# The conditioning's chunk sums: from multiply-adds on three engines to fp32 products on TensorE

## The chip, the cores and the metric

The kernel runs on one core of a Trainium2 chip. The metric is the device time of one execution in microseconds. The engines are called as the profile calls them: PE is TensorE's products and PEld its weight loads, DVE is VectorE, ACT is ScalarE, POOL is GpSimd, SP is SyncE (it issues nearly all DMAs here).

## The reference, cut to what matters

One layer of a hybrid decoder over 1024 tokens of 2048 features, all in fp32:

```python
mod = jax.nn.silu(c) @ w_ada[layer] + b_ada[layer]      # c: (1, 2048), w_ada: (2048, 6144)
shift, scale, gate = jnp.split(mod, 3, axis=-1)
h = rms_norm(x, norm_gain[layer]) * (1.0 + scale[:, None, :]) + shift[:, None, :]
proj = h @ w_in[layer]                                   # 2048 x 8192
...                                                      # eight stick-breaking, eight retention heads
y = jnp.concatenate([oa, ob], axis=-1) @ w_out[layer]
x = x + gate[:, None, :] * y
```

The change concerns the first line, for the columns of the shift and the scale: a vector of 2048 numbers times 2048 x 4096 weights, 33.5 MB that are read once.

## The kernel before, in words

**Projections.** h.T stands in SBUF in 16 blocks (kc) of 128 features by two halves (hf) of 512 tokens. Each block is kept as two exact parts, h_hi and h_lo, and so is each tile of weights (hi: a rounded copy by ScalarE, lo: the difference, by VectorE or GpSimd). `mm3` (L132 to L135) makes three products of the parts: hi hi, lo hi, hi lo.

**Order.** TensorE's order is the program's (`manual_schedule`); a scheduler orders the other engines. SyncE's queue of DMAs waits, in its own order, for the buffers that its loads fill.

**Start.** x's first four blocks of tokens are loaded, squared (L241), scaled (L257, L259) and transposed (`x_turn`, L267, copied out at L269 or L271). Meanwhile w_ada arrives in chunks of 256 columns, four tiles a chunk (`load_ada`, tag "ada", nine buffers that it shares with the raw weights of `start_w`): chunks 0 to 7 are the scale, 8 to 15 the shift. A partition p holds 16 rows of a chunk.

**Chunk sums.** `ada_sums(cc)` weighs a partition's 16 rows with silu(c) and adds them. Row 0 goes to acc_p on ScalarE (L280). Six rows (`ADA_ACT`) are scaled in place by ScalarE (L282) and added to acc_p by GpSimd (L283). Nine go to acc_d on VectorE (L285, L287), which adds acc_p at the end (L288). `ada_mod(cc)` then sums over the partitions with two products of acc_d's columns with ones (L299), and VectorE makes of that two blocks' scale (L302, L303) or shift (L305).

**First products.** `make_h(kc, hf)` makes h.T without its shift (L311 on ScalarE, L316 on VectorE). `start_w(kc)` loads a block's weights for the first seven retention heads' z and splits them: two of three low parts on GpSimd, the others on VectorE (L347). `start_mm` multiplies them into seven banks (tiles "first", half 0). In the loop over kc, the next chunk's sums stand at odd kc and `ada_mod` behind the fifth head at even kc. From kc = 10 on, transposes of x's second half go in between, in the bank "C" that mod uses as well.

**Shift.** `shifts()` runs as a task between the steps of seven projections (`unit_t`, tiles "pj_rz", half 1): load a chunk, sum it, `SHIFT_GAP` = 6 steps later `ada_mod`, then `shift_h` for two blocks of half 0. `shift_h` adds the shift (L321), rounds (L323) and takes the low part (L327, odd kc on GpSimd). After the last of these projections `shift_h` runs for half 1, while q of the first head ("pj_q") is projected. From there on come the heads and the output projection, which the change doesn't touch. `gate_part` (L501) sums the gate's columns under the heads: one fp32 product of ones (32 columns) with a 128x256 tile.

Of the kernel before, what the change touches and what calls it, by code (L numbers as in the profile page):

```python
# [11 lines left out]
F32 = mybir.dt.float32  # L12
F32R = mybir.dt.float32r
I32 = mybir.dt.int32
AF = mybir.ActivationFunctionType
ALU = mybir.AluOpType

P = 128
# [22 lines left out]
NZ = 7  # L41
ADA_BUFS = 9
ADA_ACT = (2, 4, 7, 9, 12, 14)
SHIFT_GAP = 6
# [11 lines left out]
def layer_kernel(ctx, tc, x, c, w_ada, b_ada, norm_gain, w_in, sb_q_gain, sb_k_gain, ret_norm_gain, w_out,  # L56
                 rot, ret_mask, ret_kdec, chunk_decay, out):
    nc = tc.nc
# [12 lines left out]

# [1 line left out]
    ident = cons.tile([P, P], F32, name="ident")  # L73
# [33 lines left out]
    def rsqrt_newton(y, m, u, iters=3):  # L107
        """y = m ** -0.5 from the exponent trick and Newton's iteration (u is room for a product)."""
        nc.vector.tensor_scalar(y.bitcast(I32), m.bitcast(I32), -0.5, RSQRT_MAGIC, op0=ALU.mult, op1=ALU.add)
        for _ in range(iters):  # L110
            nc.vector.tensor_tensor(u, y, y, op=ALU.mult)
            nc.vector.scalar_tensor_tensor(u, u, -0.5, m, op0=ALU.mult, op1=ALU.mult)
            nc.vector.scalar_tensor_tensor(y, u, 1.5, y, op0=ALU.add, op1=ALU.mult)

# [1 line left out]
    def split_w(raw, name, lo_eng=nc.vector):  # L116
# [19 lines left out]

    h_hi, h_lo = {}, {}  # by block of 128 features and half of the tokens

    def unit_t(col0, halves, name, lo_pool=()):
        """(w_in[:, col0:col0+128]).T @ h.T, 512 tokens a bank. Yields between its steps; returns the banks."""  # L140
        o = {hf: ps.tile([P, HALF], F32, tag="pj", bufs=4, name=f"pj_{name}_{hf}") for hf in halves}
        for kq in range(4):
            def parts(raw):
                yield raw.rearrange("p (k n) -> p k n", n=P), w_in_k[:, 4 * kq:4 * kq + 4, col0:col0 + P]
            with tc.high_priority(AHEAD):
                hi, lo = wchunk(parts, f"{name}_{kq}", nc.gpsimd if kq in lo_pool else nc.vector)
            for hf in halves:
                for k in range(4):
                    kc = 4 * kq + k
                    sl = slice(k * P, (k + 1) * P)  # L150
                    mm3(o[hf], hi[:, sl], lo[:, sl], h_hi[kc, hf], h_lo[kc, hf], kc == 0, kc == KC - 1)
                    if k % 2:
                        yield
        return o

    def unit_v(col0, name):
        """h @ w_in[:, col0:col0+256]: two heads' values, two blocks of tokens a bank."""
        o = [ps.tile([P, HALF], F32, tag="pj", bufs=4, name=f"pv_{name}_{b}") for b in range(4)]
# [16 lines left out]

    # The projections are TensorE's steady work; the heads' tasks put their small products between
    # its steps, each some steps after the one whose results it needs.
    tasks = []
# [28 lines left out]

# [1 line left out]
    # The conditioning's scale is loaded before its shift. Until the shift is known h.T stands without it,  # L209
    # and what is projected from that (the first NZ retention heads' z) gets its share later (z_bias).  # L210
    ada_rows = w_ada[0].rearrange("(p j) n -> p j n", j=16)
# [6 lines left out]
    with tc.tile_pool(name="st", bufs=1) as st:  # L218
# [7 lines left out]
        def load_ada(cc, gs=range(4)):  # L226
            """A chunk of 256 columns of w_ada: eight chunks of the scale, then eight of the shift."""
            col = (D if cc < 8 else 0) + (cc % 8) * 2 * P
# [15 lines left out]
        def x_scale(ts, ss):  # L244
            """x over its rows' root mean squares, for some blocks of tokens."""
            n = len(ts)
# [14 lines left out]
        def x_turn(kc, g, tag, bufs):  # L261
            """Half of a block of x.T, into the place that the next block of h.T's low part takes over."""
            xT[kc, g] = hp.tile([P, HALF], F32, tag=f"hl{kc}_{g}", name=f"xT{kc}_{g}")
# [8 lines left out]

        def ada_sums(cc):
            """Sums of silu(c) w_ada over a partition's sixteen rows, for a chunk of 256 columns."""
            acc_d, acc_p = [st.tile([P, 256], F32, tag=f"acc_{n}", bufs=2, name=f"acc_{n}_{cc}") for n in "dp"]
            for j in range(16):
                src = ada[cc, j // 4][:, j % 4]
                cj = silu_c[:, j:j + 1]
                if j == 0:
                    nc.scalar.activation(acc_p, src, AF.Copy, scale=cj)  # L280
                elif j in ADA_ACT:
                    nc.scalar.activation(src, src, AF.Copy, scale=cj)  # L282
                    nc.gpsimd.tensor_tensor(acc_p, acc_p, src, op=ALU.add)  # L283
                elif j == 1:
                    nc.vector.tensor_scalar(acc_d, src, cj, None, op0=ALU.mult)  # L285
                else:
                    nc.vector.scalar_tensor_tensor(acc_d, src, cj, acc_d, op0=ALU.mult, op1=ALU.add)  # L287
            nc.vector.tensor_tensor(acc_d, acc_d, acc_p, op=ALU.add)  # L288
            return acc_d

# [4 lines left out]
        def ada_mod(cc, acc):  # L295
            """Sums over the partitions: (scale + 1) gain, or shift, for two blocks of h.T."""
            mod = ps.tile([P, 2], F32, tag="C", name=f"mod_{cc}")
# [9 lines left out]
        def make_h(kc, hf):  # L307
            """h.T without its shift."""
            a, xT_kc = mods[:, kc:kc + 1], xT.pop((kc, hf))
# [9 lines left out]
        def shift_h(kc, hf):  # L319
# [4 lines left out]
            if kc == 0:  # L324
                h_lo[kc, hf] = hp.tile([P, HALF], F32R, tag=f"hl15_{hf}", name=f"h_lo0s_{hf}")
            eng = nc.gpsimd if kc % 2 else nc.vector
            eng.tensor_tensor(h_lo[kc, hf], h32, h_hi[kc, hf].bitcast(F32), op=ALU.subtract)  # L327

        starter_tags = [("A0", 1), ("A1", 1), ("B", 1)] + [("pj", 4)] * 4
        first = {}  # L330

        def start_w(kc):
# [3 lines left out]
            for i in range(2):  # L336
# [8 lines left out]
                nc.scalar.activation(hi[:, 0:n], cols, AF.Copy)  # L345
                eng = nc.gpsimd if (2 * kc + i) % 3 else nc.vector
                eng.tensor_tensor(lo[:, 0:n], cols, hi[:, 0:n].bitcast(F32), op=ALU.subtract)  # L347
                ws.append((hi, lo))
# [84 lines left out]
        def shifts():  # L433
            for cc in range(8, 16):
                if 8 < cc < 15:
                    load_ada(cc + 1)
                if cc > 8:
                    sums[cc] = ada_sums(cc)
                    yield SHIFT_GAP
# [11 lines left out]

# [1 line left out]
    hd = ctx.enter_context(ExitStack())  # L453
# [30 lines left out]
    def gate_part(h, pool):  # L484
        """The gate's columns 256 h to 256 (h + 1), without their bias, to gate_row."""
        n = 2 * P
# [21 lines left out]
    def z_bias():  # L508
        """The shift's share in the first NZ retention heads' z, to zb."""
        acc = r_tile("zb_acc")  # L510
# [23 lines left out]

# [1 line left out]
    eps_c = cons.tile([P, 1], F32, name="eps_c")  # L536
# [29 lines left out]
    def split_r(r, name):  # L566
        """A tile's two exact parts, by halves."""
        parts = [com.tile([P, S], F32R, tag="R", bufs=6, name=f"{n}_{name}") for n in ("rh", "rl")]
        return parts

    def spill_v(o, h, pool):
        """Two heads' values to DRAM, as they stand in the banks."""
        with tc.high_priority(AHEAD):
# [7 lines left out]
    def sb_attention(h, q, k, pool, gap):  # L581
        # The heads' steps: a block of 128 queries over a chunk of 512 keys. Two blocks of queries
        # go together into the product with the values.
        steps = [(0, ib, 0) for ib in range(4)]
# [54 lines left out]
        def turn(s):  # L639
            """Transposes into banks of two blocks of keys by two blocks of queries; after the second, splits."""  # L640
            half, ib, ch = steps[s]
# [61 lines left out]
    with tc.tile_pool(name="sb", bufs=1) as sb:  # L703
# [19 lines left out]

        # The first retention head's queries and keys, under the last stick-breaking head.
        o = steady(unit_t(4 * GW, (0, 1), "rq0"))
# [6 lines left out]

# [1 line left out]
    c_hi, c_lo = {}, {}  # L734
# [14 lines left out]
    def out_unit(n, tbs, name, finish, half=None, tail=2):  # L749
        """y[:, 512 n:512 (n + 1)] for some blocks of tokens, a bank each (half: of concat, to be loaded too)."""  # L750
        o = {t: ps.tile([P, HALF], F32, tag=banks[t][0], bufs=banks[t][1], name=f"y_{name}_{t}") for t in tbs}
# [28 lines left out]
    with tc.tile_pool(name="rt", bufs=1) as rt:  # L780
# [147 lines left out]

# [1 line left out]
        start(ret_attention(NH - 1, q, k, vs.pop(NH - 1), z, 2))  # L930
# [80 lines left out]
```

## Time and profile before

| | |
|---|---|
| timed runs | 2153.45, 2157.64, 2159.12 us; median 2157.64 |
| profiled execution, first to last instruction | 2156.7 us |
| its whole time | not given apart from its span; the timed median is 0.9 us above the span |
| PE busy | 2066.9 us (96%) |
| DVE, ACT, POOL busy | 1212.4 (56%), 744.9 (35%), 340.0 us (16%) |
| mean granted clock of TensorE | 0.989 |
| moved by DMA | 224.29 MB, 104 GB/s over the span |

How to read it: the profile has a row of busy time for each engine. The span in 40 slices is shown by digits, tenths of a slice. A group has its line, engine, operation, the tile it writes and those it reads, their shapes, its count, then busy time, the mean of one in ns, and the idle time of the engine just before them with what ended it. A row of waits has the waiting instruction, what ended the wait, the total in us, the number of waits and the longest. A row of the timeline has its start, its length, and the instruction. Products are pipelined, so a row of PE is longer than the time that it occupies the engine. A row of one tile has shortest, median and longest duration and the first and last start. A row of stages has the stage, its length, the busy time of each engine, the granted clock, the share of the DMA engines' time and GB/s.

### The profile page before, as it was taken

The numbers are of one execution on the slowest core, as the hardware profiler recorded it, in microseconds if no ns is written. First come the engines' busy times: TensorE is split into PE (matmuls) and PEld (weight loads), VectorE is DVE, ScalarE is ACT, GpSimd is POOL, SyncE is SP. The second block draws the span as 40 slices with busy tenths as digits, with TensorE's granted clock in tenths as the row PEclk, the third lists the DMA queues.
The fourth block names the chain that finished last, engine by engine and source line by source line (L and its number), as shares of the span: only waits on it lengthen the run. The fifth ranks groups of instructions, "written<-read, shape, count | busy, mean of one in ns | idle before, by whom it ended". The sixth has DMA issues, their size and how long they took to land.

```text
span 2156.7 us, 29735 instructions
## 1 busy us (share of the span) xinstructions
PE 2066.9 (96%) x11167; PEld 1771.6 (82%) x11167; DVE 1212.4 (56%) x2270; ACT 744.9 (35%) x1424; POOL 340.0 (16%) x475
## 2 busy tenths in 40 slices
PE   4878899999999999999999999999999999999998
PEld 3656779888988898888988988988988988688887
DVE  6999774477448653865386556556355146523132
ACT  6655442444235433543254222223232123311110
POOL 3654330111011201120111101011011010000000
PEclk9989999999999999999999999999999999999999
DMA  8847511221222112121212533433232124734132
GB/s 281 297 153 231 181 49 59 79 69 45 64 69 74 50 59 74 56 62 59 74 50 77 168 117 96 132 97 115 89 96 62 54 62 146 223 104 132 49 127 78
DMA packets 232404, 224.29 MB, mean 104 GB/s; under 512 B 12674, under 2 KB 187844, under 8 KB 232260
## 3 DMA queue, kind: packets, MB, share of 16 engines
q1 hardware_dynamic: 231872, 222.36, 32.8%
q8 instruction: 87, 1.43, 0.3%
q14 instruction: 57, 0.47, 0.1%
q10 hardware_dynamic: 388, 0.04, 0.0%
HBM read 194.03 MB, written 28.32 MB: 103 GB/s over the span
## 4 chain that ended last, share of the span: by engine, by line
PE 73%; DVE 13%; DMA 5%; issue 4%; ACT 3%; POOL 1%; ACTq 0%; SPq 0%; DVEq 0%; POOLq 0%
PE y L134 4%; PE y L135 4%; PE y L133 4%; PE pv_v L135 3%; PE pv_v L134 3%; PE pv_v L133 3%; PE pj_rq L133 3%; PE pj_rq L135 3%; PE pj_rq L134 3%; PE pj_rk L133 3%; PE pj_rk L135 3%; PE pj_rk L134 3%; PE pj_q L134 2%; PE pj_z L133 2%; PE pj_q L133 2%
## 5 line engine op out<-in xcount | busy, mean ns | idle before, releaser
L133 PE MATMUL pv_rv<-wh_rv,h_hi 128*128 128x256 f32 x512 | 146.5, 286 | 3.5 <-ACT wh_rv L119 3.5
L133 PE MATMUL y<-wh_o,c_hi 128*128 128x512 f32 x384 | 149.4, 389 | 0.0
L134 PE MATMUL y<-wl_o,c_hi 128*128 128x512 f32 x384 | 149.4, 389 | 0.0
L135 PE MATMUL y<-wh_o,c_lo 128*128 128x512 f32 x384 | 149.4, 389 | 0.0
L134 PE MATMUL pv_rv<-wl_rv,h_hi 128*128 128x256 f32 x512 | 146.1, 285 | 0.8 <-DVE wl_rv L121 0.7
L134 PE MATMUL pv_v<-wl_v,h_hi 128*128 128x256 f32 x512 | 144.9, 283 | 0.0
L133 PE MATMUL pv_v<-wh_v,h_hi 128*128 128x256 f32 x512 | 144.9, 283 | 0.0
L135 PE MATMUL pv_rv<-wh_rv,h_lo 128*128 128x256 f32 x480 | 136.4, 284 | 0.0
L135 PE MATMUL pv_v<-wh_v,h_lo 128*128 128x256 f32 x480 | 135.8, 283 | 0.0
L121 DVE TENSOR_TENSOR wl_o<-wr_o,wh_o 128x512 fp32r<-128x512 f32 x48 | 33.2, 692 | 180.3 <-ACT wh_o L119 180.3
L632 DVE TENSOR_TENSOR_SCAN om<-om 128x128 f32<-128x128 f32 (+2 forms) x96 | 96.2, 1002 | 43.6 <-POOL om L622 42.3
L119 ACT ACTIVATE wh_o<-wr_o 128x512 fp32r<-128x512 f32 x48 | 30.3, 632 | 220.7 <-PE y L135 216.3
L133 PEld LDWEIGHTS pv_rv<-wh_rv,h_hi 128*128 128x128 f32 x512 | 98.8, 193 | 4.9 <-ACT wh_rv L119 3.9
L133 PE MATMUL pj_rq<-h_hi,wh_rq 128*128 128x512 f32 x256 | 102.6, 401 | 0.3 <-ACT v L469 0.3
L133 PE MATMUL pj_rk<-h_hi,wh_rk 128*128 128x512 f32 x256 | 102.3, 400 | 0.0
L283 POOL TENSOR_TENSOR acc_p<-acc_p,ada 128x256 f32<-128x256 f32 x96 | 87.0, 907 | 96.9 <-ACT ada L282 68.0
L133 PE MATMUL pj_z<-h_hi,wh_z 128*128 128x512 f32 x256 | 101.3, 396 | 0.0
L133 PE MATMUL pj_q<-h_hi,wh_q 128*128 128x512 f32 x256 | 100.7, 393 | 0.0
L135 PE MATMUL pj_q<-h_hi,wl_q 128*128 128x512 f32 x256 | 100.6, 393 | 0.0
L134 PEld LDWEIGHTS pv_rv<-wl_rv,h_hi 128*128 128x128 f32 x512 | 98.9, 193 | 1.8 <-DVE wl_rv L121 1.6
L133 PE MATMUL pj_k<-h_hi,wh_k 128*128 128x512 f32 x256 | 100.2, 392 | 0.0
L135 PE MATMUL pj_rq<-h_hi,wl_rq 128*128 128x512 f32 x256 | 100.1, 391 | 0.0
(273 smaller groups left out, 5820.9 us busy)
## 6 DMA issues: line engine op xcount, KB each, us to landing
ada<-in_w_ada_dram SPq DMA_DIRECT2D x64, 512.0 KB
gr<-in_w_ada_dram SPq DMA_DIRECT2D x64, 256.0 KB
wr_o<-in_w_out_dram SPq DMA_DIRECT2D x48, 256.0 KB
x<-in_x_dram SPq DMA_DIRECT2D x32, 256.0 KB
wr_rz<-in_w_in_dram SPq DMA_DIRECT2D x32, 256.0 KB
wr_q<-in_w_in_dram SPq DMA_DIRECT2D x32, 256.0 KB
wr_k<-in_w_in_dram SPq DMA_DIRECT2D x32, 256.0 KB
wr_z<-in_w_in_dram SPq DMA_DIRECT2D x32, 256.0 KB
```

The source lines that it names most:

```text
L119: nc.scalar.activation(hi[:, 0:n], raw, AF.Copy)
L121: lo_eng.tensor_tensor(lo[:, 0:n], raw, hi[:, 0:n].bitcast(F32), op=ALU.subtract)
L133: nc.tensor.matmul(o, a_hi, b_hi, start=first, stop=False)
L134: nc.tensor.matmul(o, a_hi, b_lo, start=False, stop=False)
L135: nc.tensor.matmul(o, a_lo, b_hi, start=False, stop=last)
L283: nc.gpsimd.tensor_tensor(acc_p, acc_p, src, op=ALU.add)
L632: nc.vector.tensor_tensor_scan(rev, rev, rev, init, op0=ALU.mult, op1=ALU.bypass)
```

## The change

`ada_sums` no longer multiplies and adds on VectorE, ScalarE and GpSimd. A tile silu_z holds, for each of the 16 rows, 32 columns of which the first is silu(c) and the others are zero. The 16 rows of a chunk are 16 fp32 products with these 32 columns as weights; row j goes to quarter j % 4 of the 128 columns of TensorE, that is to 32 partitions of the output, and four rows are added in each quarter. VectorE copies the 128x256 sums to SBUF. `ada_mod` is as it was: the zero columns add nothing to its sum over partitions.

The products stand in TensorE's order where `ada_sums` is called: chunk 0's ahead of the first transposes, the others ahead of a block's products, in bank "C" for the scale and the first chunk of the shift, in bank "A0" for the others. All low parts of `start_w` and `shift_h` go to VectorE. SyncE's order is the same through the first products and interleaves otherwise behind them. Line numbers of the new kernel are 1 to 5 lower; comments and docstrings are gone.

```diff
-ADA_ACT = (2, 4, 7, 9, 12, 14)
...
-        def ada_sums(cc):
-            acc_d, acc_p = [st.tile([P, 256], F32, tag=f"acc_{n}", bufs=2, name=f"acc_{n}_{cc}") for n in "dp"]
+        silu_z = st.tile([P, 16, 32], F32, name="silu_z")
+        nc.vector.memset(silu_z, 0.0)
+        nc.vector.tensor_copy(silu_z[:, :, 0], silu_c)
+
+        def ada_sums(cc, tag="C"):
+            ap_ = ps.tile([P, 256], F32, tag=tag, name=f"accp_{cc}")
             for j in range(16):
-                src = ada[cc, j // 4][:, j % 4]
-                cj = silu_c[:, j:j + 1]
-                if j == 0:
-                    nc.scalar.activation(acc_p, src, AF.Copy, scale=cj)
-                elif j in ADA_ACT:
-                    nc.scalar.activation(src, src, AF.Copy, scale=cj)
-                    nc.gpsimd.tensor_tensor(acc_p, acc_p, src, op=ALU.add)
-                elif j == 1:
-                    nc.vector.tensor_scalar(acc_d, src, cj, None, op0=ALU.mult)
-                else:
-                    nc.vector.scalar_tensor_tensor(acc_d, src, cj, acc_d, op0=ALU.mult, op1=ALU.add)
-            nc.vector.tensor_tensor(acc_d, acc_d, acc_p, op=ALU.add)
-            return acc_d
+                g = j % 4
+                nc.tensor.matmul(ap_[32 * g:32 * g + 32, :], silu_z[:, j, :], ada[cc, j // 4][:, j % 4],
+                                 start=j < 4, stop=j >= 12)
+            acc = st.tile([P, 256], F32, tag="acc", bufs=2, name=f"acc_{cc}")
+            nc.vector.tensor_copy(acc, ap_)
+            return acc
...
-            eng = nc.gpsimd if kc % 2 else nc.vector
-            eng.tensor_tensor(h_lo[kc, hf], h32, h_hi[kc, hf].bitcast(F32), op=ALU.subtract)
+            nc.vector.tensor_tensor(h_lo[kc, hf], h32, h_hi[kc, hf].bitcast(F32), op=ALU.subtract)
...
-                eng = nc.gpsimd if (2 * kc + i) % 3 else nc.vector
-                eng.tensor_tensor(lo[:, 0:n], cols, hi[:, 0:n].bitcast(F32), op=ALU.subtract)
+                nc.vector.tensor_tensor(lo[:, 0:n], cols, hi[:, 0:n].bitcast(F32), op=ALU.subtract)
...
                 if cc > 8:
-                    sums[cc] = ada_sums(cc)
+                    sums[cc] = ada_sums(cc, "A0")
                     yield SHIFT_GAP
```

## The prediction

> **What bounds the kernel now.** I read the page's slices first, then the busy time by stage, then who waits for whom in each stage, and last the groups of instructions.
>
> ```profile
> span 2156.7 us, 29735 instructions
> ...
> PE   4878899999999999999999999999999999999998
> ...
> DVE  6999774477448653865386556556355146523132
> ...
> PEclk9989999999999999999999999999999999999999
> ```
>
> TensorE is full from about the fifth slice of 54 us on. Only the first five have gaps, and there VectorE is full and the granted clock drops. The change touches nothing behind them. So the stages are cut where TensorE's work changes:
>
> ```profile
> L133 PE MATMUL first<-h_hi,wh_first x112: 387/395/775, 35.5 to 162.7; 128*128 128x512 f32 x112
> L133 PE MATMUL pj_rz<-h_hi,wh_rz x112: 387/389/774, 168.1 to 267.1; 128*128 128x512 f32 x112
> ```
>
> Stage 0 goes to 35.5 us (load, norm, first chunk), stage 1 to 168.1 (the products called first), stage 2 to 267.8 (rz), stage 3 to 295.2 (q0). By stage:
>
> ```profile
> core 0: us, PE busy (x) PEld busy (x) DVE busy (x) ACT busy (x) POOL busy (x), PEclk, DMA share, GB/s
> 0.00:35.50 35.50, 8.75 (x37) 7.53 (x38) 19.29 (x62) 24.77 (x59) 7.10 (x14) 1.00 0.97 315
> 35.50:168.10 132.60, 105.22 (x461) 81.94 (x460) 119.17 (x220) 77.46 (x174) 78.13 (x77) 0.91 0.70 229
> 168.10:267.80 99.70, 88.29 (x372) 72.01 (x371) 84.61 (x128) 48.70 (x95) 40.31 (x40) 0.91 0.63 199
> 267.80:295.20 27.40, 24.99 (x97) 18.48 (x96) 22.54 (x27) 13.19 (x22) 13.11 (x9) 0.94 0.16 47
> sum 295.20, PE 227.25 PEld 179.97 DVE 245.61 ACT 164.12 POOL 138.65; mean PE 56.81 PEld 44.99 DVE 61.40 ACT 41.03 POOL 34.66
> ```
>
> VectorE works 119 of stage 1's 133 us and 85 of stage 2's 100. TensorE is idle for 27 and 11 us, and its mean clock is 0.91. What it waits for (the first three rows from stage 1, the next from stage 2, the last from stage 0's timeline):
>
> ```profile
> PE first L135 <- POOL wl_first L347: 7.9, 4, 3.1
> PE xtp L267 <- DVE x L259: 7.1, 2, 5.4
> PE xtp L267 <- DVE xT L269: 3.8, 2, 2.1
> ```
> ```profile
> PE mod L299 <- DVE acc_d L288: 11.4, 4, 5.2
> ```
> ```profile
> 31.39 0.98 PE L299 MATMUL mod<-ones,acc_d 128*128 128x1 f32 x4 [3.83 <-DVE acc_d L288]
> ```
>
> So the chunk sums do hold TensorE up, directly and through a late VectorE. But TensorE has little idle time to give, and that is the question of this change.
>
> **What goes, and what comes.** Groups of the first 300 us:
>
> ```profile
> L287 DVE SCALAR_TENSOR_TENSOR acc_d<-ada,silu_c,acc_d 128x256 f32<-128x256 f32 x128 | 94.3, 742 | 1.1
> L283 POOL TENSOR_TENSOR acc_p<-acc_p,ada 128x256 f32<-128x256 f32 x96 | 87.0, 907 | 96.9 <-ACT ada L282 68.0 <-issue 19.9 <-ACT acc_p L280 3.8
> L282 ACT ACTIVATE ada<-ada,silu_c 128x256 f32<-128x256 f32 x96 | 43.0, 497 | 5.3 <-DMA ada<-in_w_ada_dram 5.3
> L347 POOL TENSOR_TENSOR wl_first<-wr_first,wh_first 128x384 fp32r<-128x384 f32 (+1 forms) x21 | 26.7, 1291 | 3.7 <-ACT wh_first L345 3.7
> L327 POOL TENSOR_TENSOR h_lo<-h,h_hi 128x512 fp32r<-128x512 f32 x16 | 24.9, 1554 | 54.9 <-ACT h_hi L323 54.7
> L269 DVE COPY xT<-xtp 128x512 f32<-128x512 f32 x16 | 10.9, 683 | 3.0 <-PE xtp L267 3.0
> L321 DVE SCALAR_TENSOR_TENSOR h<-h_hi,shift,h_lo 128x512 f32<-128x512 f32 x32 | 27.3, 886 | 3.6 <-POOL h_lo L327 3.6
> L285 DVE TENSOR_SCALAR acc_d<-ada,silu_c 128x256 f32<-128x256 f32 x16 | 9.6, 601 | 0.0
> L327 DVE TENSOR_TENSOR h_lo<-h,h_hi 128x512 fp32r<-128x512 f32 x14 | 9.6, 683 | 0.0
> L288 DVE TENSOR_TENSOR acc_d<-acc_d,acc_p 128x256 f32<-128x256 f32 x16 | 9.0, 565 | 1.7 <-POOL acc_p L283 1.4
> L280 ACT ACTIVATE acc_p<-ada,silu_c 128x256 f32<-128x256 f32 x16 | 8.0, 498 | 4.7 <-DVE acc_d L288 4.5 <-DMA ada<-in_w_ada_dram 0.2
> ```
>
> VectorE loses 94.3 + 9.6 + 9.0 = 113 us and ScalarE 51. GpSimd loses all of its 139. VectorE gains 16 copies of the sums out of PSUM: 128x256, between half of L269's 683 ns and all of it, so 5 to 11, taken as 8. It gains the 21 low parts that GpSimd split, up to 0.683 us each (L327), 14, and GpSimd's 16 low parts of the shifted h, 11. VectorE comes to 246 - 113 + 33 = 166 of 295 us, and it no longer bounds. These edits cost nothing while TensorE is the longer engine; in stage 3 that cover is thin (below).
>
> **The new cost is TensorE's**: 16 chunks of 16 fp32 products, 32 columns of weights by 256 columns. Before has this very shape once per gate part (gp), between its usual products:
>
> ```profile
> 1295.15 0.39 PE L134 MATMUL pj_rk<-h_lo,wh_rk 128*128 128x512 f32 x1
> 1295.38 0.39 PE L135 MATMUL pj_rk<-h_hi,wl_rk 128*128 128x512 f32 x1
> 1295.70 0.62 PE L501 MATMUL gp<-ga,ones 128*32 128x256 f32 x2
> 1296.25 0.50 PE L133 MATMUL pj_rk<-h_hi,wh_rk 128*128 128x512 f32 x1
> 1296.59 0.39 PE L134 MATMUL pj_rk<-h_lo,wh_rk 128*128 128x512 f32 x1
> ```
>
> A usual product occupies 0.23 us (1295.15 to 1295.38), though its row says 0.39. One fp32 product leaves two records: 0.62 less one record's 0.38 puts the second 0.24 behind the first. From 1295.38 to 1296.59 there are 1.21 us; less two usual products, 0.46, and two records, 0.48, 0.27 is left, the price of going into 32-column weights and back. So a chunk costs 0.27 plus its 32 records:
> - one behind another: 32 x 0.24 + 0.27 = 7.95 us;
> - all four quarters at once: 8 x 0.24 + 0.27 = 2.2 us;
> - in pairs: the two records of one product share a quarter and follow each other, as in gp, but the next product's first record, in another quarter, runs beside the second. That makes 17 steps: 17 x 0.24 + 0.27 = 4.35 us.
>
> No row of before has two quarters in succession, so 2.2 and 7.95 are the ends. I take the pairs: gp's row shows that the second record of a quarter starts only when the first is through, and every row of this trace starts in the program's order; with both, the next quarter can't start before that second record has.
>
> The Trainium skill's page "TensorE: Matmul & The Clock Gate" (section "Part 3: Packing small matmuls — row/col tiling") says that matmuls start and end in program order, and gives 2.38 times for three column tiles; no run here shows either yet. By the ratio alone a chunk would be 7.68 / 2.38 + 0.27 = 3.5 us, an estimate, and the sum below 13 us lower.
>
> Counts for the stages, and the price of a transpose and of a mod (stage 1):
>
> ```profile
> 163.52 1.03 PE L267 MATMUL xtp<-ident,x 128*128 128x128 f32 x8
> ```
> ```profile
> L267 PE MATMUL xtp<-ident,x 128*128 128x128 f32 x97 | 15.6, 296 | 16.2 <-DVE x L259 7.1 <-DVE xT L269 3.8 <-ACT xT L271 2.7
> L299 PE MATMUL mod<-ones,acc_d 128*128 128x1 f32 x28 | 4.0, 247 | 0.1
> ```
>
> Eight transposes in 1.03 us with the last at 0.27 are 0.11 each.
>
> - **Stage 0**: the first chunk's sums run on TensorE as its tiles land, ahead of the transposes that wait for x anyway. The 3.83 us wait of mod goes: -4 (-2 to -5).
> - **Stage 1**: 3 x 112 products x 0.23 = 77, 97 transposes 11, seven mods 3: 91. Sums of chunks 1 to 8: 8 x 4.35 = 35. The waits for GpSimd and for x go. For what is late next I put 6: sums, mods and late transposes take turns in one PSUM bank, whose wait for xT was 3.8 with VectorE 90% busy, and TensorE now stands in order behind the landing of w_ada, with the first products queued behind it. 91 + 35 + 6 = 132 against 132.6: -1.
> - **Stage 2**: 77 + 3 for mods + 7 x 4.35 = 30 + 3 for such waits = 113 against 99.7: +14. Here TensorE was already busy 88 us, and the wait that goes is 11.4 plus the low clock.
> - **Stage 3**: VectorE does every low part. For each of 16 blocks it adds the shift (0.683 us as L327, or 0.886 as L321 with GpSimd beside it) and takes the low part (0.683), and it splits q's weights four times: 25 to 28 us, against 27.4 now, when GpSimd took 1.55 apiece for half of the low parts: 0 (-2 to +2).
>
> Sum: -4 - 1 + 14 + 0 = +9. The span is 2156.7 and the timed median 2157.6 (0.9 around it): **2166 us**. In general the change is -56 + 15 x chunk, so it breaks even at a chunk of 3.75 us.
>
> DMA. Stage 1 and stage 2 moved:
>
> ```profile
> DMA packets 25203, 30.35 MB, mean 229 GB/s; under 512 B 1161, under 2 KB 20862, under 8 KB 25194
> ```
> ```profile
> DMA packets 25819, 19.89 MB, mean 199 GB/s; under 512 B 890, under 2 KB 24640, under 8 KB 25811
> ```
>
> Stage 0 moved 315 GB/s. At that rate 30.35 and 19.89 MB are 96 and 63 us, below any stage time here, so loads are hidden. SyncE's order through stage 1 is unchanged; its tiles come free when TensorE has read them. In stage 2 w_ada and rz's weights interleave otherwise, and one late tile stops both: that is in the 3 us, up to 10.
>
> **Rivals.**
> - *Four quarters at once* (this one ends faster). Place: the chunk sums. Price: 2.2 us a chunk, -56 + 33 = -23: 2135 us. It decides once a chunk is under 3.75. For it: the order of the products goes round the quarters. Against: gp's two records 0.24 apart on one quarter. The Trainium skill's page "TensorEngine Tiling (Array Packing)" (section "Tiling Modes") states this rule: with 32 columns there are four tiles that operate independently and execute in parallel; no row of before has a second tile to test it.
> - *No overlap*: the change doesn't do what its quarters say. 7.95 us a chunk, -56 + 119 = +63: 2221 us. For it: the only rows of this shape show 0.24 a record, and weights and products of fp32 have never run side by side here. Against: nothing but that the quarters are separate columns.
> - *A new wait*: pairs as forecast, but TensorE stands for w_ada's tiles and its clock falls as it does now (0.91). That gives back up to 10 us: 2176, inside the forecast's own range.
>
> **How the numbers follow.** Pairs 0.50, four at once 0.20, no overlap 0.30. The likeliest one's own range is 2152 to 2178 (records at 0.23 rather than 0.24 take 15 x 17 x 0.01 = 3 off; waits about 10 either way). The whole range reaches from 2134, the middle of four at once, to 2223, past the middle of no overlap: about 0.10 + 0.49 + 0.21 = 0.8. 0.3% is 6.5 us, about what a measurement of this kernel can tell. Pairs: slower 0.60, same 0.28, faster 0.12; four at once: faster 0.93; no overlap: slower 1. Together faster 0.25, same 0.15, slower 0.60.
>
> **What would show it.** In the changed profile: records of accp 0.12 us apart on the mean (pairs), 0.06 (four) or 0.24 (none); rz starting near 164 and q0 near 277; VectorE under 70% in stages 1 and 2; no wait of mod for acc; stage 3 still some 27 us. Wrong would be a stage 2 that isn't longer than 100 us, waits of accp for w_ada above 10 us, or a difference that arises behind 300 us.

## The result, and the profile after

The new kernel is faster: 2122.24 us (median; 2119.81 to 2122.84) against 2157.33 us (2153.45 to 2159.12), a ratio of 0.984, 95% interval 0.9826 to 0.9854. The forecast of 2166 us had the wrong sign. The profiled execution took 2122.75 us. Its page, the rows that answer to those of before, and GpSimd's:

```profile
span 2120.8 us, 30239 instructions
...
PE   5999999999999999999999999999999999999998
...
DVE  4664662768166826783575556466354156513132
...
POOL 0000000111021102110211112011011010000000
PEclk9999999999999999999999999999999999999999
```

TensorE is full from the second slice on (before: from the fifth), the granted clock never drops, VectorE is no longer full anywhere near the start, and GpSimd hardly works in the first seven slices, 371 us. The stages, cut as before, with the same columns:

```profile
0.00:31.66 31.66, 9.93 (x70) 6.01 (x70) 13.53 (x54) 21.02 (x50) 0.70 (x6) 1.00 0.93 300
31.66:141.67 110.01, 108.28 (x717) 82.97 (x717) 64.48 (x160) 52.79 (x109) 0.00 (x0) 1.00 0.88 294
141.67:235.66 93.99, 93.99 (x595) 73.83 (x594) 48.98 (x82) 33.60 (x57) 0.00 (x0) 1.00 0.66 208
235.66:259.94 24.28, 23.24 (x98) 17.63 (x96) 22.58 (x35) 13.34 (x23) 0.10 (x1) 1.00 0.22 64
259.94:2120.80 1860.86, 1839.01 (x10207) 1591.38 (x10205) 967.68 (x1835) 580.39 (x1077) 201.18 (x335) 1.00 0.28 87
```

| stage | before, us | after, us | difference | forecast |
|---|---|---|---|---|
| 0: load, norm, first chunk | 35.5 | 31.7 | -3.8 | -4 |
| 1: first products | 132.6 | 110.0 | -22.6 | -1 |
| 2: rz | 99.7 | 94.0 | -5.7 | +14 |
| 3: q0 | 27.4 | 24.3 | -3.1 | 0 |
| the rest | 1861.5 | 1860.9 | -0.6 | 0 |

The second row is the one to read: TensorE does more instructions in stage 1 than before (717 against 461 records) in less time, and is busy for 108.3 of 110.0 us. What is left of its waits, first in the start, then over stages 1 and 2 (all of the rows):

```profile
PE accp L282 <- DVE ss L246: 11.0, 1, 11.0
PE rows_ps L97 <- DMA rows<-in_ret_norm_gain_dram: 8.8, 1, 8.8
PE accp L282 <- DMA ada<-in_w_ada_dram: 1.1, 3, 0.4
```
```profile
PE first L132 <- ACT h_hi L308: 0.9, 1, 0.9
PE xtp L266 <- ACT xT L270: 0.7, 1, 0.7
PE accp L282 <- DVE xT L268: 0.7, 1, 0.7
PE first L133 <- DVE h_lo L313: 0.3, 1, 0.3
```

Over the 204 us of stages 1 and 2 these waits come to 2.6 us (1.7 by busy time, as the ends of products are modelled). None of it is for w_ada and none for a mod. Now the question on which the forecast hung, a chunk of sums on TensorE between two usual products:

```profile
47.77 0.40 PE L134 MATMUL first<-h_hi,wl_first 128*128 128x512 f32 x1
48.10 1.93 PE L282 MATMUL accp<-ada,silu_z 128*32 128x256 f32 x32
49.97 0.50 PE L132 MATMUL first<-h_hi,wh_first 128*128 128x512 f32 x1
50.30 0.40 PE L133 MATMUL first<-h_lo,wh_first 128*128 128x512 f32 x1
```

From 47.77 to 50.30 are 2.53 us. Less two usual products of 0.23, the 32 records and the switching take **2.07 us**: four records at once, not the pairs of 4.35 us. In the trace's single records the four of a wave start 7 ns apart, a wave begins 0.216 to 0.240 us behind the one before it, and the last of eight waves begins 1.535 us behind the first. So it is in all 15 chunks of stages 1 and 2.

### The profile page after: what moved, and what is told of

It reads as the page before. It is cut to its first block, busy times and chain, and to the rows that moved or that the text cites. A ratio compares the mean times of both kernels' runs of the same rounds, so it can differ in the third digit from the quotient of the medians.

```text
span 2120.8 us, 30239 instructions
## 1 busy us (share of the span) xinstructions
PE 2074.5 (98%) x11679; PEld 1771.8 (84%) x11679; DVE 1117.3 (53%) x2165; ACT 701.1 (33%) x1312; POOL 202.0 (10%) x342
## 3 DMA queue, kind: packets, MB, share of 16 engines
q8 instruction: 91, 1.49, 0.3%
## 4 chain that ended last, share of the span: by engine, by line
PE 83%; DVE 8%; DMA 5%; ACT 3%; issue 2%; POOL 0%; SPq 0%; ACTq 0%; DVEq 0%; POOLq 0%
PE y L132 4%; PE y L133 4%; PE y L134 4%; PE pv_v L134 3%; PE pv_v L133 3%; PE pv_v L132 3%; PE pj_rq L132 3%; PE pj_rq L134 3%; PE pj_rq L133 3%; PE pj_q L133 3%; PE pj_rk L132 3%; PE pj_rk L134 3%; PE pj_rk L133 3%; PE pj_q L134 3%; PE pj_q L132 3%; PE pj_z L132 2%
## 5 line engine op out<-in xcount | busy, mean ns | idle before, releaser
L134 PE MATMUL pj_rk<-h_hi,wl_rk 128*128 128x512 f32 x256 | 99.9, 390 | 0.0
```

What stands on the lines that cost most here:

```text
L134: nc.tensor.matmul(o, a_lo, b_hi, start=False, stop=last)
```

## The experiments

Two theories were set against each other first. One (Q in the texts on record) says that the quarters run side by side, each with its own queue, so that a chunk costs the records of its longest quarter, 0.22 us each, and 0.27 for switching, and that TensorE's sum makes the time. The other (O) keeps the forecast's step: records start in the program's order, so one that waits for its quarter holds up the next quarter's. Where GpSimd is concerned, theory G says that its work beside VectorE's makes VectorE's own instructions longer, so that its splits cost more than their own time. All twelve runs together; the stages are those of the profiled execution:

| run | median, us | ratio (95%) | stages 0, 1, 2, 3, us |
|---|---|---|---|
| e1_one_quarter | 2199.84 | 1.0209 (1.0194 to 1.0224) | 32.2, 151.7, 129.9, 24.3 |
| e2_two_quarters | 2146.74 | 0.9961 (0.9946 to 0.9975) | 30.1, 125.5, 105.8, 24.6 |
| e3_pair_order | 2121.92 | 0.9847 (0.9832 to 0.9861) | 30.1, 112.4, 94.2, 24.3 |
| e4_gpsimd_splits | 2125.68 | 0.9865 (0.985 to 0.9879) | 30.6, 113.7, 94.0, 27.4 |
| e5_old_sums_no_gpsimd_splits | 2142.60 | 0.9936 (0.9915 to 0.9957) | 34.7, 128.4, 91.8, 24.4 |
| e6_four_rows | 2106.03 | 0.9767 (0.9751 to 0.9783) | 31.3, 101.4, 84.8, 24.6 |
| e7_old_two_rows | 2106.65 | 0.9769 (0.975 to 0.9789) | 28.5, 109.1, 81.5, 27.5 |
| e8_share4 | 2116.70 | 0.9819 (0.9803 to 0.9835) | 30.0, 108.7, 92.4, 24.6 |
| e9_share8 | 2114.76 | 0.9807 (0.9792 to 0.9822) | 31.2, 109.1, 88.5, 24.2 |
| e10_old_two_rows_no_gpsimd | 2098.82 | 0.9735 (0.972 to 0.9749) | 28.8, 102.8, 80.3, 24.3 |
| e11_runs_of_four | 2165.01 | 1.0041 (1.0026 to 1.0056) | 31.4, 133.6, 114.0, 24.3 |
| e12_old_sums_gpsimd_idle | 2139.99 | 0.9928 (0.9912 to 0.9945) | 35.4, 118.4, 98.5, 24.3 |

The kernel before took 2155.0 to 2155.4 us beside them. E6, E7 and E10 leave rows of the sums out, to show a limit. Stages 0 and 1 are best read together: the new kernel and E3 have the same work there and differ by 1.6 us in the one and by 2.4 the other way in the other, but only by 0.8 in the sum (141.7 and 142.5 us).

### How many quarters: E1 and E2

```diff
-                g = j % 4
+                g = j % 1      # E1; j % 2 in E2
...
-                                 start=j < 4, stop=j >= 12)
+                                 start=j < 1, stop=j >= 16 - 1)      # E2: j < 2, j >= 16 - 2
-            nc.vector.tensor_copy(acc, ap_)
+            acc = accs[cc % 2]      # zeros outside the quarters that are used
+            nc.vector.tensor_copy(acc[0:32], ap_[0:32])      # E2: 0:64
```

> All 16 products of a chunk go to the same quarter of TensorE's columns; the other quarters' sums stay zero. Theory Q (the changed kernel gains because records of different quarters run at once, 8 waves of 0.22 us a chunk, and TensorE is the bound): 32 records of 0.22 us one behind another, 7.2 us a chunk with the 0.27 us of switching instead of 2.1, 15 chunks on the path, 77 us more than 2122: 2199 us. Rival V (what counts is that VectorE and GpSimd are relieved; TensorE has gaps that hide its sums): under 2160 us.

> The 16 products of a chunk alternate between two quarters. Theory Q: 16 waves of 0.22 us and 0.27 of switching, 3.7 us a chunk, 15 x 1.65 = 25 us more than 2122: 2147 us, still faster than before, so that the break-even of 3.75 us a chunk that the prediction put is wrong. If that break-even holds: 2157 us, as before. Rival V: 2122 to 2130 us.

Both came out as theory Q has it, 2199.84 and 2146.74 us. A chunk in E1 and in E2, in TensorE's timeline:

```profile
34.69 0.40 PE L134 MATMUL first<-h_hi,wl_first 128*128 128x512 f32 x1
35.02 7.09 PE L285 MATMUL accp<-ada,silu_z 128*32 128x256 f32 x32
42.04 1.97 PE L266 MATMUL xtp<-ident,x 128*128 128x128 f32 x16
```
```profile
47.95 0.40 PE L134 MATMUL first<-h_hi,wl_first 128*128 128x512 f32 x1
48.28 3.65 PE L285 MATMUL accp<-ada,silu_z 128*32 128x256 f32 x32
51.85 0.50 PE L132 MATMUL first<-h_hi,wh_first 128*128 128x512 f32 x1
52.19 0.40 PE L133 MATMUL first<-h_lo,wh_first 128*128 128x512 f32 x1
```

The rows of the sums shorten from 7.09 to 3.65 to 1.93 us with one, two and four quarters: 32, 16 and 8 steps of 0.22 and the last record's 0.38. In E1 the last record starts 6.715 us behind the first, 0.217 a step, so one quarter never runs two records at once.

The whole times give the price of a step on the path. From E1 to the new kernel 24 steps a chunk go and 77.6 us, so 3.23 us a step: 15 chunks at 0.216. So each microsecond of the sums costs a microsecond, in all 15 chunks that stand among full work. That part of the forecast's formula, 15 x chunk, holds. Its constant doesn't: E2's chunk costs 52.19 - 47.95 - 0.46 = 3.78 us, the forecast's break-even, and E2 is 0.4% faster than before.

### In which order: E3 and E11

```diff
-                g = j % 4
+                g = j // 2 % 4      # E3: two products of a quarter in succession; E11: j // 4, four
...
-                                 start=j < 4, stop=j >= 12)
+                                 start=j in (0, 2, 4, 6), stop=j in (9, 11, 13, 15))      # E11: j % 4 == 0, j % 4 == 3
```

> Same products, four quarters, but two products of the same quarter in succession (quarter j // 2 % 4). Theory Q in its strong form (each quarter takes its own records when it is free, whatever stands in front in the program's order): 2122 us, 8 waves of four. Theory O (the prediction's: a record does not start before the one in front of it has started, and a quarter's record waits for the quarter): four records of a quarter in succession, of which one runs beside the next quarter's first, 25 steps of 0.22 us, 5.7 us a chunk, 54 us more: 2176 us. In between, if only a few records can be passed.

> Same products, four quarters, but four products of the same quarter in succession (quarter j // 4), so that a quarter's first record stands eight records behind the quarter's in front. Theory Q in its strong form: records pass others of another quarter as far as TensorE's queue reaches, but now each quarter reads another of the chunk's four tiles: 2122 us, starts of a wave some 27 us apart in thousandths (7 to 13 ns were seen for two and four records). If only a few records are passed: up to 2180 us.

E3, where the program has four records of one quarter in succession, is as fast as the new kernel:

```profile
46.21 0.40 PE L134 MATMUL first<-h_hi,wl_first 128*128 128x512 f32 x1
46.53 1.97 PE L282 MATMUL accp<-ada,silu_z 128*32 128x256 f32 x32
48.44 0.50 PE L132 MATMUL first<-h_hi,wh_first 128*128 128x512 f32 x1
48.78 0.40 PE L133 MATMUL first<-h_lo,wh_first 128*128 128x512 f32 x1
```

The row of the sums is 1.97 us long, 1.93 in the new kernel, again with four records a wave; those of the first wave start 0, 14, 27 and 40 ns behind the first. One quarter never runs two at once (E1), so these four belong to four quarters, and the fifth, ninth and thirteenth record of the program start ahead of the second. **Theory O falls.** E11 puts eight records of a quarter in succession:

```profile
50.21 0.40 PE L134 MATMUL first<-h_hi,wl_first 128*128 128x512 f32 x1
50.54 4.59 PE L282 MATMUL accp<-ada,silu_z 128*32 128x256 f32 x32
55.06 0.50 PE L132 MATMUL first<-h_hi,wh_first 128*128 128x512 f32 x1
55.40 0.39 PE L133 MATMUL first<-h_lo,wh_first 128*128 128x512 f32 x1
```

That is 4.73 us a chunk, and 2165 us, so only a few records can be passed. The first 0.27 us of a chunk show the difference, in the new kernel (all engines, from 34.50 us on) and in E11 (from 50.53 us on); the last number of a row counts its records in that window:

```profile
34.51 0.64 PE L282 MATMUL accp<-ada,silu_z 128*32 128x256 f32 x8
```
```profile
50.54 0.62 PE L282 MATMUL accp<-ada,silu_z 128*32 128x256 f32 x2
```

Eight records have started there, two here. In E11's trace the first four steps have one record each; the fifth comes together with a second one (at 0.887 and 0.893 us); the pairs go on, and the last four are alone again: 20 steps, the last start at 4.215 us. All 15 chunks of stages 1 and 2 show the same. This is what comes out if each quarter has room for four records, one that runs and three that wait: records leave in the program's order, each into its own quarter, and hold up those behind them only when that quarter's room is full. The fifth record gets in when the first is through, at step 4 the next quarter's first follows, and so on: 4 alone + 12 pairs + 4 alone. The same rule gives eight full waves for j % 4 and for j // 2 % 4. It is fitted to three orders; a room of four wasn't measured in another way.

The Trainium skill's page "TensorE: Matmul & The Clock Gate" (section "Part 3: Packing small matmuls — row/col tiling") calls the start of matmuls a strict FIFO. E3 disagrees: by the program three more records of the first quarter stand ahead of the second quarter's first, which starts 14 ns behind the first record of all. The measurement decides. The page "TensorEngine Tiling (Array Packing)" (section "Tiling Modes"), by which tiles execute in parallel, agrees with E1, E2 and the new kernel: 32, 16 and 8 steps.

### GpSimd's splits: E4, E5 and E12

E4 is the new kernel with GpSimd's low parts back; E5 is the kernel before with its low parts on VectorE; E12 is E5 with all 15 rows of the sums on VectorE as well (row 0 stays on ScalarE), so that GpSimd does nothing in these stages.

```diff
# E4, against the new kernel, and the same for start_w
-            nc.vector.tensor_tensor(h_lo[kc, hf], h32, ...)
+            eng = nc.gpsimd if kc % 2 else nc.vector
+            eng.tensor_tensor(h_lo[kc, hf], h32, ...)
# E5, against the kernel before, and the same for start_w
-            eng = nc.gpsimd if kc % 2 else nc.vector
-            eng.tensor_tensor(h_lo[kc, hf], h32, ...)
+            nc.vector.tensor_tensor(h_lo[kc, hf], h32, ...)
# E12, E5 and this
-ADA_ACT = (2, 4, 7, 9, 12, 14)
+ADA_ACT = ()
```

> The sums on TensorE as in the changed kernel, but GpSimd takes its low parts of the first weights and of the shifted h again, as before. Theory Q: TensorE bounds the first two stages either way; only q0's stage, where VectorE is busy throughout, changes, by its 3 us: 2122 to 2127 us. Rival G (the gain comes from GpSimd's slow splits, which the first products waited for 7.9 us, and from what GpSimd's work does to VectorE's): 2135 us or more.

> The kernel before, sums by multiply-adds as they were, with only the low parts of the first weights and of the shifted h moved from GpSimd to VectorE. Theory Q: VectorE bounds the first two stages and gets 21 x 0.62 + 16 x 0.68 = 24 us more, of which 13 + 5 lie in these stages: 2157 + 10 to 20 = 2167 to 2177 us. Rival G: less contention and no wait for GpSimd outweigh that: 2150 us or less.

> The kernel before without GpSimd in its start: rows 1 to 15 of the sums all on VectorE, the low parts too, row 0 on ScalarE. Contention theory (VectorE's multiply-adds take 0.74 us with GpSimd at work beside them and 0.48 without): 224 multiply-adds of 0.48 are 108 us where 128 of 0.74 were 94, so 96 rows more cost VectorE only 14 us, the low parts 24, and its other operations get 6 us shorter: 2142.6 + 28 - 6 = 2155 to 2165 us, about as before. If GpSimd's help was real work taken off VectorE: 96 x 0.62 = 60 us more than 2142.6, 2190 us or more.

**E4** lost 3.4 us against the new kernel, within theory Q's 2122 to 2127 us and far from rival G's 2135. In its trace stage 3 is 27.4 us again, with GpSimd busy for 13 of them:

```profile
238.30:265.70 27.40, 23.93 (x97) 17.36 (x96) 22.53 (x27) 13.19 (x22) 13.11 (x9) 1.00 0.16 47
```

So once the sums are on TensorE, the splits matter in stage 3, where GpSimd needs some 1.49 us for a low part and TensorE waits 2.6 us for them. The first two stages take up to 2.6 us more (144.3 us, against 141.7 in the new kernel and 142.5 in E3, from one trace each).

**E5** went against theory Q. VectorE was nearly full and got more to do, and the kernel became 13 us faster, in rival G's range (2150 us or less). **E12** gave VectorE 96 multiply-adds more, and it was faster still by 2.6 us, within the noise of the two. That is 15 us under the least that the contention theory expected. The multiply-adds (group of VectorE in the first 300 us) in E5, then in E12; before's 128 took 742 ns each:

```profile
L287 DVE SCALAR_TENSOR_TENSOR acc_d<-ada,silu_c,acc_d 128x256 f32<-128x256 f32 x128 | 78.7, 621 | 0.9
```
```profile
L287 DVE SCALAR_TENSOR_TENSOR acc_d<-ada,silu_c,acc_d 128x256 f32<-128x256 f32 x224 | 101.2, 478 | 0.6
```

On the mean the same instruction takes 478 ns with GpSimd idle, 621 with GpSimd's row sums beside it, 742 with its splits too. So 128 x 0.478 = 61 of before's 94.3 us are the work itself, and 33 us come from beside it: 128 x (0.742 - 0.621) = 15.5 with the splits, which alone differ between before and E5, and 18 with the row sums. In E12 ScalarE's scaling of the six rows went together with GpSimd's adds, but the single rows of the traces tell the two apart. Of before's 128 multiply-adds, 51 have no instruction of GpSimd beside them: they take 478 ns on the mean, and the 13 of them with ScalarE at work throughout take 481. The 77 beside GpSimd take 917. In E5 it is 60 with 477 and 68 with 748. So the lengthening goes with GpSimd, not with ScalarE. Copies out of PSUM don't show it: those of 128x512 (L269) take 683 ns beside GpSimd and 684 without. The 96 rows that GpSimd adds in E5 save VectorE 101.2 - 78.7 = 22.5 us of multiply-adds beside E12, 0.23 a row, half of what they take alone. Even that is lost on VectorE's other instructions. Up to the end of stage 3 VectorE is busy for 245.6 us in before, and in E5 and E12, where it does GpSimd's splits and then all that GpSimd did, for 239.2 and 233.2 (DVE):

```profile
sum 279.30, PE 221.25 PEld 176.58 DVE 239.22 ACT 163.73 POOL 87.67; mean PE 55.31 PEld 44.14 DVE 59.80 ACT 40.93 POOL 21.92
```
```profile
sum 276.60, PE 219.37 PEld 177.25 DVE 233.17 ACT 128.37 POOL 0.84; mean PE 54.84 PEld 44.31 DVE 58.29 ACT 32.09 POOL 0.21
```

The Trainium skill's page "SBUF — State Buffer" (section "Who interferes with whom") says that a VectorE instruction with two SBUF inputs contends with a GpSimd instruction that reads SBUF. The multiply-adds here, which have two inputs in SBUF, agree with it; they don't show how the one engine holds up the other. The multiplication of L285, which reads one tensor and a scalar a partition, takes 346 ns alone and 856 beside GpSimd, so two tensors aren't needed for it.

Stage 1 of E5 shows the same thing from TensorE's side:

```profile
34.70:163.10 128.40, 104.38 (x459) 82.58 (x460) 117.29 (x241) 78.81 (x177) 51.73 (x60) 0.91 0.76 243
```

VectorE does 241 instructions in 117.3 us here, and did 220 in 119.2 us before. With the sums still on it, VectorE is the bound all the same, and the granted clock is still 0.91.

### What bounds next: E6, E7 and E10

E6 is the new kernel with four rows of each chunk instead of sixteen. E7 is the kernel before with two rows, E10 the same with the low parts on VectorE.

```diff
# E6, against the new kernel
-            for j in range(16):
-                g = j % 4
+            for j in range(0, 16, 4):      # with start=True, stop=True
+                g = j // 4
# E7, against the kernel before, and E10, against E5
-            for j in range(16):
+            for j in (0, 1):
```

> The changed kernel with only rows 0, 4, 8 and 12 of each partition's sixteen in the sums, one product to each quarter; the other twelve are loaded and left out. Theory Q (TensorE bounds, so its sums cost what they occupy): two waves instead of eight, 6 x 0.216 = 1.3 us a chunk less, 15 chunks, 19 us: 2103 us. Rival V (gaps hide the sums): 2118 to 2122 us.

> The kernel before with only rows 0 and 1 of the sixteen in the sums, one on ScalarE, one on VectorE, and their sum; the other fourteen are loaded and left out. It shows what the multiply-adds cost where they stood, without TensorE's new work. Theory Q: the changed kernel less its sums, 2122 - 15 x 2.1 = 2091 us, and 3 to 8 us more for GpSimd's splits: 2094 to 2099 us. By the prediction's sum (waits of 56 us go): 2101 us. Rival V: about 2122, since the sums on TensorE would cost nothing.

> The kernel before with only rows 0 and 1 of the sixteen in the sums, and with the low parts of the first weights and of the shifted h on VectorE: sums nearly free, GpSimd idle at the start. It tells what was left of the start without sums. Theory Q: 2106.6 less q0's stage (3 us) and less the waits behind GpSimd: 2100 to 2103 us, no lower, because the first products' stage then has the loads as its bound (30 to 32 MB at 318 GB/s, 95 to 101 us). If only TensorE's work bounds it: 2091 us.

E6 takes 16.2 us off the new kernel where 15 chunks of six steps less make 19, so rival V (no gain) falls. E10, at 2098.82, is 1 to 4 us under its expectation, and 8 above what TensorE alone would allow. E7, at 2106.65, was 8 to 13 us above theory Q's expectation and 6 above the prediction's sum: in its trace TensorE still waits for VectorE and ScalarE in stage 1 (4.1 us for x, 2.6 for xT, 2.2 for h_lo), its mean clock is 0.95, and GpSimd splits for 27 us. Taking the sums away altogether would not have shown the limit of this stage; the splits had to go as well. Stage 1 of E6 and of E10:

```profile
31.30:132.70 101.40, 98.52 (x524) 76.56 (x525) 63.28 (x160) 52.42 (x108) 0.00 (x0) 1.00 0.95 318
```
```profile
28.80:131.60 102.80, 95.16 (x461) 76.86 (x461) 66.37 (x173) 57.09 (x121) 0.00 (x0) 0.98 0.96 326
```

Both stop near 102 us with the DMA engines busy for 95% of the time, at 318 and 326 GB/s, and E10 with no sums to speak of isn't shorter than E6. In E6 TensorE is nearly full itself (98.5 of 101.4 us). In E10 it is idle for 7.6 us, and its waits are put down to VectorE and ScalarE (the longest 2.6 us for x, then 2.1 for wh_first), none to a DMA. So stage 1 can give some 8 us more. That the loads are the bound behind it is likely by their rate, but no run took loads away to show it.

### A part of the rows back to VectorE: E8 and E9

```diff
+            for j in range(m):      # m = 4 in E8, 8 in E9
+                src, cj = ada[cc, j // 4][:, j % 4], silu_c[:, j:j + 1]
+                if j == 0:
+                    nc.vector.tensor_scalar(acc, src, cj, None, op0=ALU.mult)
+                else:
+                    nc.vector.scalar_tensor_tensor(acc, src, cj, acc, op0=ALU.mult, op1=ALU.add)
-            for j in range(16):
+            for j in range(m, 16):
...
-            nc.vector.tensor_copy(acc, ap_)
+            nc.vector.tensor_tensor(acc, acc, ap_, op=ALU.add)
```

> The changed kernel with rows 0 to 3 of a chunk's sixteen given back to VectorE (one multiplication and three multiply-adds, then an addition of TensorE's sums in place of the copy), twelve rows on TensorE: six waves for eight. Theory Q: 2 x 0.216 x 15 = 6.5 us less: 2116 us, as VectorE is busy for 64 of 110 us and 49 of 94 us in the first two stages and gets 2 us a chunk. Rival: VectorE's sums come late for mod or its queue delays h: 2122 us or more.

> The changed kernel with rows 0 to 7 of a chunk's sixteen given back to VectorE, eight on TensorE: four waves for eight. Theory Q: 4 x 0.216 x 15 = 13 us less than 2122: 2109 us. Rival W (VectorE, at 64 of 110 us in the stage of the first products, gets 3.7 us a chunk, 30 us, and is full and late again, or the loads, which ran at 318 GB/s with the four-row sums, become the bound): 2112 to 2120 us.

Both beat the two kernels, E8 as theory Q had it and E9 within rival W's range: 2116.70 and **2114.76 us, a ratio of 0.9807** (0.9792 to 0.9822, and 0.9826 to 0.9854 for the change as it stands). E9 takes four of eight steps off 15 chunks, 13 us, and gains 7.5. Its stages 1 and 2:

```profile
31.20:140.30 109.10, 103.35 (x589) 79.96 (x589) 89.02 (x231) 51.69 (x106) 0.00 (x0) 0.98 0.91 305
140.30:228.80 88.50, 87.95 (x484) 70.23 (x483) 67.84 (x131) 34.62 (x59) 0.00 (x0) 1.00 0.66 209
```

Stage 2 gives 5.5 of the 6.0 us that seven chunks of four steps make. Stage 1 gives 0.9 of 6.9, or 1.4 with stage 0: VectorE is back at 89 of 109 us, the loads at 305 GB/s, and TensorE waits ahead of transposes again (2.6 us for x from VectorE, 2.0 for xT from ScalarE). Whether VectorE or the loads decide there wasn't tried.

## Why the prediction was wrong, point by point

- **The failed step** is the choice of the pairs: "with both, the next quarter can't start before that second record has", 4.35 us a chunk. A chunk costs 2.07. From rows in which every start follows the program I concluded that starts must follow it. But in those rows each product shares columns with the one before; nothing could have overtaken. In the new kernel the first records of four quarters start within 20 ns, ahead of the first quarter's second record (0.24 us). E3 shows that the order of starts gives way where the quarters differ, and E11 where that ends. At 15 chunks this step is 15 x 2.28 = 34 us of the 44 between 2166 and 2122.
- **The rival** of four quarters at once had the mechanism, at 0.20. It gave 2135 us; 13 us were still missing. Two come from the chunk, 2.07 instead of 2.2, the rest from two terms of the sum.
- **The allowance for waits** (6 us in stage 1, 3 in stage 2) was wrong: TensorE is idle 1.7 us in stage 1 and not at all in stage 2. With the measured chunk, the prediction's terms give 91 + 17 + 6 = 114 and 80 + 14 + 3 = 97 us, against 110.0 and 94.0. I added waits for VectorE and for the bank as they were with VectorE 90% full, and it is at 59% now (64.5 of 110). E8 and E9 fit this: with VectorE at 71% and 82% of stage 1, TensorE is idle there for 3.3 and 5.8 us.
- **Stage 3** was costed at 0 (-2 to +2) and gave -3.1, also in E5 and E12, which share only the moved low parts with the new kernel; E4, which hasn't moved them, has 27.4 us. The shift's add and the low part take 747 and 686 ns there, within what the forecast took. But I summed whole durations, 1.37 to 1.57 us a block; in VectorE's timeline the adds of successive blocks start 1.27 us apart (238.29, 239.56, 240.83), so 16 blocks take 20.3 us, and four splits of weights at 0.61 from start to start 2.4. TensorE is busy for 23.2 of the 24.3 us. Before, a low part on GpSimd took 1.55 us, every second time.
- **GpSimd's price to VectorE** was not in the sum. I counted 113 us that leave VectorE and 33 that come, at before's durations, and those were lengthened by GpSimd beside them: the shift's add took 886 ns and takes 748 (L318), and h_lo's scaling took 935 (L316 in before) and takes 748 (L313). In E12, with the sums on VectorE and GpSimd idle, they take 745 and 744. A copy of the sums takes 420 ns (L285), within the half to all of 683 that I allowed; its size is the reason there, not GpSimd.

```profile
L313 DVE SCALAR_TENSOR_TENSOR h_lo<-xT,mods,h_hi 128x512 fp32r<-128x512 f32 x32 | 23.9, 748 | 4.5 <-ACT h_hi L308 3.4
L318 DVE SCALAR_TENSOR_TENSOR h<-h_hi,shift,h_lo 128x512 f32<-128x512 f32 x32 | 23.1, 748 | 0.5 <-DMA zraw<-zt 0.2
L285 DVE COPY acc<-accp 128x256 f32<-128x256 f32 x16 | 6.7, 420 | 5.3 <-PE accp L282 5.2
```

  Taking the splits off GpSimd brought E5's 13 us in before; 3 of them are stage 3's, where TensorE had waited for GpSimd's own low parts, so the 13 aren't the lengthening alone. In the new kernel it is mostly covered, since TensorE bounds (E4: 3.4 us): the two halves of the change overlap. The sums alone bring 29 us (E4), the splits alone 13 (E5), both 35.
- **The constant** of -56 should have been -66: the measured -35 less 15 x 2.07. So the break-even is a chunk of 66 / 15 = 4.4 us, and E2 (3.78, faster by 0.4%) and E11 (4.73, slower by 0.4%) stand on its two sides. By this line pairs would have made no difference that can be measured (4.35: -1 us).
- **Right** were: stage 0 (-3.8 against -4, so close in part by luck, since E3 with the same start has 30.1 us for 31.7); VectorE no longer bounds, and mod's wait is gone; switching at 0.27 (2.07 less eight steps of 0.22 leaves 0.31) and 0.22 to 0.24 a record; that TensorE's time for the sums is paid in full, with nothing to hide it (E1's slope); that the loads don't hold the new kernel up; and that nothing changes behind 300 us.
- **The low clock** went together with the waits. Before, 64 products in stages 1 to 3 were 0.43 us apart instead of 0.23; now it is one. Whether the gaps in TensorE's work bring the clock down wasn't tried by itself; the runs with the lowest clock in stage 1, 0.91 (before, E5, E12), are those in which TensorE is idle there for more than 16 us, and E7 with 11.5 us has 0.95.

## What to carry to other kernels

Small products that use a quarter of TensorE's columns can cost a quarter, if neighbours in the program's order go to different quarters: spread them round, and keep runs in one quarter short (two products of fp32 in succession cost 2.11 us a chunk against 2.07, four cost 4.73). Before pricing a move between engines from the durations of a trace, ask which of them are lengthened by a neighbour: of VectorE's 94 us of multiply-adds here a third came from GpSimd's work beside them. And don't price an overlap from rows in which no overlap was possible; there, both ends deserve like chances.

## What the runs showed that was not expected

- Records of different quarters start out of the program's order: four within 40 ns in E3, with a room that fits four records a quarter (E3, E11).
- An fp32 product of 32 columns by 256 occupies its quarter for 2 x 0.217 us (E1), and four quarters run fully side by side: 8 steps in 1.555 us plus the last record.
- VectorE's 128x256 multiply-add takes 478, 621 or 742 ns on the mean as GpSimd is idle, adds, or adds and splits (E12, E5, before). With all of GpSimd's work moved to it, VectorE was busy for 12 us less in the first four stages (233.2 for 245.6).
- A part of the sums on VectorE and a part on TensorE is the fastest of the versions that do all of the work, 2114.76 us, though VectorE alone bounded the kernel before.
